# Hybrid decoder layer on one core: the first 512 streamed columns of w_in as four row pieces of full width, multiplied as each block of tokens arrives

## Chip, cores and metric

The kernel runs on one core of a Trainium2 chip. The metric is the device time of one execution in microseconds (us); lower is better. A core has a TensorE (PE), a VectorE (DVE), a ScalarE (ACT), a GpSimd (POOL), and queues that start transfers, of which SyncE's (SP) carries the weights.

## The reference, cut to what matters

One decoder layer for 512 tokens of width 1024. The normalised tokens are multiplied with one wide matrix `w_in`; its column groups are the queries, the keys and values of three attention branches (compressed, selected, window), gates, and the inputs of an mLSTM. The compressed branch reads the keys and values of 31 overlapping blocks of 32 tokens, adds a position row, and sends them through two small matrices.

```python
h = rmsnorm(x, g_mix)                        # x * rsqrt(mean(x*x) + EPS) * g
z = h @ w_in                                 # split by IN_SIZES:
# q 512 | kc 128, vc 128 | ks 128, vs 128 | kw 128, vw 128 | gates 24 | mLSTM ...
def compress_blocks(tok_g, w1, w2, pe):
    idx = CMP_STRIDE * jnp.arange(n_cmp)[:, None] + jnp.arange(CMP_LEN)[None, :]
    blk = tok_g[:, :, idx] + pe
    flat = blk.reshape(b, g, n_cmp, CMP_LEN * d)
    return jax.nn.gelu(flat @ w1) @ w2
```

Behind them come attention, mLSTM, a mixture of 16 experts and per-layer embeddings. The change touches none of these; they take the time from about 70 us to the end.

## The kernel before, in words

**Tokens.** The 512 tokens are four blocks `b` of 128. Each block of x (`xs`) is loaded, its sum of squares formed by ScalarE (`square`), its scale by a chain of small VectorE operations (`rstd` for one block, `rstd_cols` for blocks 2 and 3 at once), and VectorE multiplies it by scale and g_mix (line 372). g_mix is one row (`grow`) that TensorE spreads over 128 partitions (`gmb`, line 320). `rows_t` then transposes the block by eight TensorE transposes into the PSUM tiles `tp` (line 376), and `parts` copies these into a high part `hTh` (ScalarE, line 383) and a rest `hTl` (VectorE, line 385).

**Weights.** `Stream` brings the pieces of `w_in` and of the compression weights (`w_ck`, `w_cv`) in a fixed order into four raw buffers (`rawWR`), and splits each into a high part `whWS` (ScalarE, lines 97 and 103) and a rest `wlWS` (VectorE, lines 100 and 106, or POOL, line 108) in one of four split buffers. A split buffer is free again when the last product with it is done. Each product of the reference is three TensorE products: hTh·wh, hTl·wh, hTh·wl.

**The steps and their order.** `ORDER` lists the pieces: `z2` (kc and vc, columns 512 to 767), `z3` (ks and vs, 768 to 1023), `z4` (kw, vw, gates; 288 columns, three pieces by rows), `z0`, `z1` (queries), and `c0`, `c1`, the first compression product for keys and for values, four pieces each. z2 and z3 are two pieces each: 512 rows by 256 columns. z2 is multiplied block by block while the blocks arrive (`tok_mm_late`, `z2_mm`); z3 follows for all four blocks at once. What is done with a finished step is in generators that are advanced between the pieces: `finish_c2` copies z2 (`zt`), turns it (rope), transposes it on TensorE (line 526), copies that to `TT` (lines 532, 534), adds the position rows (`tb`, line 580), and splits the result into `bhl` (lines 581, 582), which `c0` (line 589) reads. `z1_out` does it for the keys and values of z3 and z4 (`kz`, `v`, line 547; key transposes, line 557; `khh`, `kll`). `angles` makes the tables for rope (`trig`), for which ScalarE loads another function table and POOL negates a part; POOL then starts the transfer of `w2s`, which VectorE copies to `w2d` (line 569).

**PSUM.** The pool `PM` has three banks named `mm`, `PA` two each of `tp` and `S`, `PO` one `o`. z2 adds up in two `mm` banks, z3 in two `S` banks, z4 in two of each: it can start in a bank only when that bank's former content has been read.

`after(x)` and `issue_after(x)` only fix an order: what stands under them comes behind x in the program. Line numbers of the profile are those of the kernel it belongs to.

Of the kernel before, what the change touches and what calls it, by code (L numbers as in the profile page):

```python
# [19 lines left out]
P = 128  # L20
S = 512
# [111 lines left out]
def tile_hybrid(ctx, tc, x, p, positions, g_mix, w_in, b_if, w_ck1, w_ck2, pe_ck, w_cv1, w_cv2, pe_cv,  # L133
# [157 lines left out]
    def z1_acc(c):  # L291
        names = {2: ["mm"] * 2, 3: ["S"] * 2, 4: ["mm", "mm", "S", "S"], 0: ["mm"] * 2, 1: ["S"] * 2}[c]
        acc = [(PM if nm == "mm" else PA).tile([P, 512], F32, name=nm) for nm in names]
        if c == 4:
            return acc, [t[:, :288] for t in acc]
        return acc, [acc[b // 2][:, (b % 2) * 256:(b % 2) * 256 + 256] for b in range(NB)]

    acc2 = z1_acc(2)
    with tc.tile_pool(name="start", bufs=1) as sp:
# [54 lines left out]

        def z2_mm(b):
            for h in range(2):
                with tc.issue_after(tr_.ins) if h else nullcontext():
                    tok_mm(acc2[1], 4 * h, 4 * h + 4, *w2_[h], 256, 2, [b])
# [79 lines left out]
        tpc = PM.tile([P, 512], F32, name="mm")  # L438
        T.transpose(tpc[:, :92], rows, ident[:92, :92])
# [49 lines left out]
    def z1_mm(c, h, dst):  # L489
        with tc.issue_after(front_.ins) if (c, h) == (3, 0) else nullcontext():  # L490
            wh, wl = st.get(("z", c, h))
        if c == 4:
            tok_mm(dst, *K4[h], wh, wl, 288, 1)
        else:
            tok_mm(dst, 4 * h, 4 * h + 4, wh, wl, 256, 2)

    def z1_out(c, acc, j):
        for _ in range(1):
# [19 lines left out]
            elif c == 2:  # L518
                z = zp.tile([P, 2, 256], F32, name="zt")
                A.activation(z, acc[j].rearrange("p (b n) -> p b n", b=2), AF.Copy)  # L520
                rope(z[:, :, 0:128].rearrange("p b (h d) -> p b h d", h=2), j, 2, zp)
# [13 lines left out]
            else:  # L535
# [121 lines left out]
    def begin(g, wait):  # L657
        next(g)
        later.append([wait, g, wait])

    for o in ORDER:
        c = int(o[1])
        if o[0] == "z":
            h = done_z.get(c, 0)
            done_z[c] = h + 1
            if h == 0:
                accs[c] = z1_acc(c) if c != 2 else acc2
            if c != 2:
                z1_mm(c, h, accs[c][1])
                advance(5)  # L670
            if h == (2 if c == 4 else 1):
                if c == 2:
                    begin(finish_c2(), WAIT[0])
                else:
                    for j in range(2):
                        begin(z1_out(c, accs[c][0], j), WAIT[1])
                if c == 4:
                    nsa_gates()
# [1015 lines left out]
```

## Time and profile before

| | us |
|---|---|
| median of 3 runs (lowest to highest) | 709.89 (709.51 to 711.25) |
| the profiled execution | 711.02 |
| its span in the profile | 709.3 |
| PE busy in the span | 684.3 |
| DVE busy | 563.2 |
| ACT busy | 436.0 |
| POOL busy | 130.4 |

The span is that of the profiled execution; the difference between it and the 711.02 lies around the span. Busy times of several engines overlap. An engine's share is a mean over stages that have different limits: of the 709 us, the change concerns the first 70.

### The profile page before, as it was taken

How to read it: one execution, taken by the hardware profiler on the slowest of the kernel's cores; microseconds unless marked ns; L12 is line 12 of the kernel's file. 1: busy time of each engine (PE TensorE's matmuls, PEld its weight loads, DVE VectorE, ACT ScalarE, POOL GpSimd, SP SyncE). 2: the span in 40 equal slices, each digit the busy share in tenths (PEclk: the TensorE clock that was granted, in tenths of full speed). 3: DMA queues.
4: the chain of work that ended last, by engine and by line, in shares of the span. 5: the costliest groups of instructions: out<-in, count | busy, mean ns of one | idle time of the engine just before them, and what ended most of it. 6: DMA issues, size and time to landing. Idle time of an engine off the chain costs nothing.

```text
span 709.3 us, 11568 instructions
## 1 busy us (share of the span) xinstructions
PE 684.3 (96%) x3913; PEld 584.6 (82%) x3913; DVE 563.2 (79%) x1427; ACT 436.0 (61%) x848; POOL 130.4 (18%) x184
## 2 busy tenths in 40 slices
PE   7989989999999999999999999999999999999995
PEld 5989976889999998888888888876788888887784
DVE  5877989888777758888884673668999999986986
ACT  6447746576666666665553332326999999986642
POOL 5010023333334220000000001222222222110000
PEclk9999999999999999999999999999999999999998
DMA  8424551222121212332219438944999999607511
GB/s 267 124 73 140 167 140 32 85 65 61 31 60 30 61 31 64 87 79 71 83 38 354 146 119 266 375 154 157 388 394 362 355 329 365 245 31 269 191 63 60
DMA packets 83152, 113.72 MB, mean 160 GB/s; under 512 B 9553, under 2 KB 52129, under 8 KB 83090
## 3 DMA queue, kind: packets, MB, share of 16 engines
q1 hardware_dynamic: 73344, 97.14, 41.3%
q0 software_dynamic: 5648, 11.53, 4.5%
q10 hardware_dynamic: 4098, 4.30, 1.8%
q8 instruction: 31, 0.51, 0.3%
q14 instruction: 31, 0.25, 0.1%
HBM read 108.41 MB, written 12.58 MB: 171 GB/s over the span
## 4 chain that ended last, share of the span: by engine, by line
PE 79%; DVE 8%; DMA 6%; ACT 4%; issue 2%; POOL 1%; ACTq 0%; POOLq 0%; DVEq 0%
PE mm L945 12%; PE S L1476 11%; PE mm L271 10%; PE mm L1648 6%; PE mm L1501 6%; PE mm L1117 6%; PE mm L768 3%; PE mm L1281 3%; PE S L271 2%; PE tp L862 2%; DMA wr<-in_w_re 2%; PE S L841 2%; PE tp L1462 2%; DVE wlWS L106 1%; ACT whWS L103 1%
## 5 line engine op out<-in xcount | busy, mean ns | idle before, releaser
L106 DVE TENSOR_TENSOR wlWS<-rawWR,whWS 128x1024 fp32r<-128x1024 f32 (+2 forms) x78 | 89.5, 1153 | 28.6 <-ACT whWS L103 27.5
L103 ACT ACTIVATE whWS<-rawWR 128x1024 fp32r<-128x1024 f32 (+2 forms) x79 | 82.3, 1050 | 43.0 <-PE S L271 8.5
L106 DVE TENSOR_TENSOR wlWS<-rawWE,whWS 128x1024 fp32r<-128x1024 f32 x58 | 69.1, 1221 | 3.7 <-ACT whWS L103 2.4
L103 ACT ACTIVATE whWS<-rawWE 128x1024 fp32r<-128x1024 f32 x58 | 60.6, 1071 | 5.1 <-PE S L1476 4.5
L271 PE MATMUL mm<-whWS,hTl 128*128 128x256 f32 (+1 forms) x200 | 59.3, 296 | 1.4 <-DVE hTl L385 1.4
L271 PE MATMUL mm<-wlWS,hTh 128*128 128x256 f32 (+1 forms) x200 | 59.1, 296 | 0.0
L271 PE MATMUL mm<-whWS,hTh 128*128 128x256 f32 (+1 forms) x200 | 59.1, 296 | 0.0
L945 PE MATMUL mm<-hTh,whWS 128*128 128x512 f32 x128 | 50.3, 393 | 0.0
L945 PE MATMUL mm<-hTh,wlWS 128*128 128x512 f32 x128 | 50.0, 391 | 0.0
L945 PE MATMUL mm<-hTl,whWS 128*128 128x512 f32 x128 | 50.0, 391 | 0.0
L852 POOL TENSOR_SCALAR pr<-pr,sm 128x128 f32<-128x128 f32 (+3 forms) x64 | 35.2, 564 | 78.1 <-DVE sm L850 36.4
L1476 PE MATMUL S<-whWS,tgh 128*128 128x512 f32 x120 | 48.6, 405 | 0.0
L1476 PE MATMUL S<-wlWS,tgh 128*128 128x512 f32 x120 | 47.8, 398 | 0.1
L1476 PE MATMUL S<-whWS,tgl 128*128 128x512 f32 x120 | 47.3, 394 | 0.0
L846 ACT ACTIVATE pr<-pr,sm 128x128 f32<-128x128 f32 (+3 forms) x64 | 35.4, 555 | 16.9 <-DVE sm L844 16.8
L271 PEld LDWEIGHTS mm<-whWS,hTl 128*128 128x128 f32 x200 | 38.6, 193 | 1.7 <-DVE hTl L385 1.6
L271 PEld LDWEIGHTS mm<-wlWS,hTh 128*128 128x128 f32 x200 | 38.6, 193 | 0.0
L271 PEld LDWEIGHTS mm<-whWS,hTh 128*128 128x128 f32 x200 | 38.5, 193 | 0.1
L108 POOL TENSOR_TENSOR wlWS<-rawWR,whWS 128x384 fp32r<-128x384 f32 (+1 forms) x17 | 24.8, 1460 | 72.4 <-ACT whWS L103 67.5
L865 ACT ACTIVATE ph<-tp 128x512 fp32r<-128x512 f32 (+1 forms) x48 | 25.1, 523 | 20.4 <-PE tp L862 20.1
L842 DVE CUSTOM_DVE_ANT_0 pr<-S,strip 128x128 f32<-128x128 f32 (+3 forms) x64 | 29.3, 485 | 3.9 <-PE S L841 3.4
L1506 POOL DMA_INDIRECT y_dram<-ye,gidx x16 | 20.8, 1299 | 61.9 <-ACT aeh L1490 58.8
(490 smaller groups left out, 2076.6 us busy)
## 6 DMA issues: line engine op xcount, KB each, us to landing
rawWE<-in_w_e SPq DMA_DIRECT2D x59, 512.0 KB, 9.9
rawWR<-in_w_in SPq DMA_DIRECT2D x40, 512.0 KB, 3.9
mT<-in_w_e SPq DMA_DIRECT2D x22, 512.0 KB, 12.6
rawWR<-in_w_e SPq DMA_DIRECT2D x13, 512.0 KB, 10.4
rawWR<-in_w_out SPq DMA_DIRECT2D x8, 512.0 KB, 4.3
yy<-y_dram SPq DMA_DIRECT2D x8, 512.0 KB, 5.4
rawWR<-in_w_ck SPq DMA_DIRECT2D x4, 512.0 KB, 3.9
rawWR<-in_w_cv SPq DMA_DIRECT2D x4, 512.0 KB, 5.4
```

The lines of the kernel that those rows point to most:

```text
L103: self.last_hi = self.nc.scalar.activation(h[:, :n], flat, AF.Copy)
L106: self.last = self.nc.vector.tensor_tensor(l[:, :c], flat[:, :c], h[:, :c].bitcast(F32), OP.subtract)
L271: T.matmul(dst[b], a[:, kk, b * P:(b + 1) * P], w[:, kk - k0, :n], start=(kk == 0 and i == 0 and b % share == 0), stop=(kk == NK - 1 and i ...
L842: V.tensor_tensor_reduce(pr[:, hh, :n], s_[:, :n], strip[:, 512 - q0:640], 0.125, -3.0e38, OP.add, OP.max, sm[:, 0, hh:hh + 1])
L846: A.activation(pr[:, hh, :n], pr[:, hh, :n], AF.Exp, bias=sm[:, 1, hh:hh + 1], accum_out=sm[:, 2, hh:hh + 1])
L852: G.tensor_scalar(pr[:, hh, :n], pr[:, hh, :n], sm[:, 3, hh:hh + 1], 1.0, op0=OP.mult, op1=OP.mult)
L865: A.activation(ph[:, :nj], tp[:, :nj], AF.Copy)
L945: T.matmul(ps, w[:, k], a[:, k], start=(k == 0 and i == 0), stop=(k == NK - 1 and i == 2))
L1117: T.matmul(ps, w[:, k, f * P:(f + 1) * P], a[:, k], start=(k == 0 and i == 0), stop=(k == 3 and i == 2))
L1476: T.matmul(ps, a[:, 2 * m + k], w[:, k], start=(m == 0 and k == 0 and i == 0), stop=(m == 3 and k == 1 and i == 2))
L1501: T.matmul(acc[c], a[:, k], w[:, 0, c * 512:(c + 1) * 512], start=(k == 0 and i == 0), stop=(k == 1 and i == 2))
L1648: T.matmul(acc, a[:, k], w[:, 0, lo:hi], start=(k == 0 and i == 0), stop=(k == NK - 1 and i == 2))
```

## The change

The 512 columns of z2 and z3 are now four pieces `zz` 0 to 3 of 256 rows by 512 columns. `zz_mm` multiplies one of them with one block into the accumulator `accz[b]` (two `mm`, two `S`), 512 wide. All of it happens as the blocks arrive, so z2 and z3 no longer stand in `ORDER`, and their outputs (`finish_c2`, `z1_out(3)`) are begun ahead of z4. The low halves of zz0, zz1 and zz2 are POOL's, that of zz3 VectorE's; before, only that of z2's first piece was POOL's. The row of g_mix is now started second on SP's queue, before it was second on ScalarE's. Ten transposes on nothing (`keep_warm`, before 14) are made ahead of the g_mix products instead of behind them, and `gmb` lies in an `mm` and an `o` bank. The two small transposes for `trig` and `cols` go to `tp` banks. zt is copied in four pieces 256 wide, before two of 512.

```diff
-N_WARM = 14
+N_WARM = 10
...
-ORDER = "z2 z2 z3 z3 z4 z4 c0 z4 c0 c0 z0 c0 z0 c1 z1 c1 z1 c1 c1".split()
+ORDER = "z4 z4 c0 z4 c0 c0 z0 c0 z0 c1 z1 c1 z1 c1 c1".split()
...
+    for m in range(4):
+        st.add(("zz", m), [(0, 512, wall[:, 2 * m:2 * m + 2, 512:1024])], [P, 2, 512], *first)
...
+    def zz_mm(b, m, terms):
+
+        wh, wl = zw[m]
         for i in terms:
             a, w = ((hTh, wh), (hTl, wh), (hTh, wl))[i]
-            for kk in range(k0, k1):
-                m = T.matmul(dst[b], a[:, kk, b * P:(b + 1) * P], w[:, kk - k0, :n],
-                         start=(kk == 0 and i == 0 and b % share == 0),
-                         stop=(kk == NK - 1 and i == 2 and b % share == share - 1), skip_group_check=True)
-        return m
+            for kk in range(2):
+                last = T.matmul(accz[b], a[:, 2 * m + kk, b * P:(b + 1) * P], w[:, kk], start=(m == 0 and i == 0 and kk == 0),
+                                stop=(m == 3 and i == 2 and kk == 1), skip_group_check=True)
+        return last
...
-    acc2 = z1_acc(2)
+    accz, zw = z1_acc(4)[0], []
...
-                A.dma_start(grow, g_mix)
+                nc.sync.dma_start(grow, g_mix)
             if b < 2:
                 st._load()
-        keep_warm(N_WARM)
-
-        gmb = [PA.tile([P, 512], F32, name="S") for _ in range(2)]
+                st._load()
+        gm_ = keep_warm(N_WARM)
+
+        gmb = [PM.tile([P, 512], F32, name="mm"), PO.tile([P, 512], F32, name="o")]
         for c in range(2):
-            T.matmul(gmb[c], ones, grow[:, c * 512:(c + 1) * 512], start=True, stop=True)
+            with after(gm_):
+                gm_ = T.matmul(gmb[c], ones, grow[:, c * 512:(c + 1) * 512], start=True, stop=True)
...
-            w2_.append(st.get(("z", 2, 0)))
+            for m in range(2):
+                zw.append(st.get(("zz", m)))
+        ps0, xs_, tr_ = rows_t(0, None, gm_)
+        with after(st.last_hi):
+            hi_, lo_ = parts(0, ps0, None)
+        with after(hi_):
+            sq_ = square(1)
+        with after(lo_):
+            rstd(rst[:, 1:2], ss[:, 1:2], sp)
+        with after(sq_):
+            zw.append(st.get(("zz", 2)))
+        st.late_low = []
+        with after(st.last_hi):
+            zw.append(st.get(("zz", 3)))
+        (low_,), st.late_low = st.late_low, None
+        st.pool_from, st.split_ahead = D, 1
...
         with after(st.last_hi):
-            sq_ = square(1)
-        ps0, xs_, tr_ = rows_t(0, None)
-        with after(xs_):
-            made = rstd(rst[:, 1:2], ss[:, 1:2], sp)
-        with after(sq_):
-            hi_, lo_ = parts(0, ps0, made)
-        st.late_low = []
-        with after(hi_):
-            w2_.append(st.get(("z", 2, 1)))
-        (low_,), st.late_low = st.late_low, None
-        st.pool_from, st.split_ahead = D, 1
-        with after(st.last_hi):
-            for b in (2, 3):
-                sq_ = square(b)
-        tok_mm_late(acc2[1], 0, 4, *w2_[0], 256, 2, 0, (0, 1, 2))
-        m_ = tok_mm_late(acc2[1], 4, 8, *w2_[1], 256, 2, 0, (0, 1))
+            sq_ = square(2)
+        for i in range(3):
+            for m in range(2):
+                zz_mm(0, m, (i,))
+        for i in range(3):
+            m_ = zz_mm(0, 2, (i,))
         ps1, xs_, tr_ = rows_t(1, lo_, m_)
         with after(xs_):
-            xs_ = low_()
+            low_ = low_()
         with after(tr_):
-            tok_mm_late(acc2[1], 4, 8, *w2_[1], 256, 2, 0, (2,))
-        with after(xs_):
-            made = rstd_cols(rst[:, 2:4], ss[:, 2:4], sp, 2)
+            zz_mm(0, 3, (0, 1, 2))
         with after(sq_):
-            hi_, lo_ = parts(1, ps1, made)
+            hi_, lo_ = parts(1, ps1, low_)
+        with after(hi_):
+            square(3)
+        with after(lo_):
+            rstd_cols(rst[:, 2:4], ss[:, 2:4], sp, 2)
         for b in (2, 3):
-            psb, xs_, tr_ = rows_t(b, lo_ if b == 2 else xs_)
-            z2_mm(b - 1)
-            hi_, lo_ = parts(b, psb, None)
+            psb, xs_, tr_ = rows_t(b, lo_)
+            for m in range(4):
+                with after(tr_ if m > 1 else None):
+                    zz_mm(b - 1, m, (0, 1, 2))
+            hi_, lo_ = parts(b, psb, xs_)
         with after(lo_):
             trig = angles()
-        z2_mm(NB - 1)
+        for m in range(4):
+            zz_mm(NB - 1, m, (0, 1, 2))
         front_ = lo_
...
-                A.activation(z, acc[j].rearrange("p (b n) -> p b n", b=2), AF.Copy)
+                for b in range(2):
+                    A.activation(z[:, b], acc[2 * j + b][:, 0:256], AF.Copy)
...
-        gens = [z1_out(2, accs[2][0], j) for j in range(2)]
+        gens = [z1_out(2, accz, j) for j in range(2)]
...
+    begin(finish_c2(), WAIT[0])
+    for j in range(2):
+        begin(z1_out(3, accz, j), WAIT[1])
```

TensorE, around the transposes of block 1 (tile `tp` from `xs`). Before, with block 0: `mm` is z2's accumulator, `wh`/`wl` numbers 154/155 are z2's first piece, 196/197 its second.

```order
L282 MATMUL mm_92<-whWS_196,hTh_76 128x256 [waits Activation_49]
...
L282 MATMUL mm_92<-whWS_196,hTl_77 128x256 [waits DVE_49]
...
L376 MATMUL tp_227<-ident_78,xs_109 128x128 [waits DMAHW5_49,DVE_49,PE_49]
...
L282 MATMUL mm_92<-wlWS_197,hTh_76 128x256 [waits DVE_49]
...
L271 MATMUL mm_92<-whWS_154,hTh_76 128x256 [waits Activation_49]
```

The same place after the change; the numbers of `wh`/`wl` are 152/153 for zz0, 159/160 for zz1, 193/194 for zz2, 199/200 for zz3.

```order
L286 MATMUL mm_92<-wlWS_153,hTh_76 128x512 [waits Pool_49]
L286 MATMUL mm_92<-wlWS_153,hTh_76 128x512
L286 MATMUL mm_92<-wlWS_160,hTh_76 128x512 [waits Pool_49]
L286 MATMUL mm_92<-wlWS_160,hTh_76 128x512
L286 MATMUL mm_92<-whWS_193,hTh_76 128x512 [waits Activation_49]
L286 MATMUL mm_92<-whWS_193,hTh_76 128x512
L286 MATMUL mm_92<-whWS_193,hTl_77 128x512 [waits DVE_49]
L286 MATMUL mm_92<-whWS_193,hTl_77 128x512
L286 MATMUL mm_92<-wlWS_194,hTh_76 128x512 [waits Pool_49]
L286 MATMUL mm_92<-wlWS_194,hTh_76 128x512
L375 MATMUL tp_234<-ident_78,xs_113 128x128 [waits DMAHW6_49,DVE_49,PE_49]
```

The transposes of block 1 stood ahead of the last low half's products; now they stand behind the products with POOL's third low half.

TensorE, from z4 to c0, after the change: `mm_510`, `mm_511`, `S_512`, `S_513` are z4's accumulators for blocks 0 to 3, `tp_604` the c2 transposes, `tp_672` the key transposes, `mm_758` z0's accumulator, `o_627` c0's.

```order
L274 MATMUL mm_510<-whWS_514,hTh_76 128x288 [waits Activation_49]
...
L274 MATMUL mm_511<-whWS_514,hTh_76 128x288 [waits DVE_49]
...
L274 MATMUL S_512<-whWS_514,hTh_76 128x288 [waits DVE_49,PE_49]
...
L536 MATMUL tp_604<-ident_78,zt_456 128x128 [waits DMAHW0_49,DMASW0_49,PE_49]
...
L567 MATMUL tp_672<-ident_78,qs_490 128x128 [waits DVE_49,PE_49]
...
L274 MATMUL mm_758<-whWS_744,hTh_76 128x256 [waits Activation_49]
...
L599 MATMUL o_627<-whWS_562,bhl_454 128x256 [waits DVE_49]
...
L599 MATMUL o_627<-whWS_760,bhl_454 128x256 [waits Activation_49]
L274 MATMUL mm_758<-wlWS_745,hTh_76 128x256 [waits DVE_49]
```

Before, the c2 transposes stood behind z3 and ahead of all of z4; now 72 of z4's 96 products come first, and c0's first product follows 24 products of z4, the key transposes and four products of z0 later.

VectorE, after the change, where z4's banks come free: `mm_92`, `mm_93`, `S_94`, `S_95` are `accz` 0 to 3, `v1` the values of z3, `wlWS_629` the low half of z4's third piece.

```order
L106 TENSOR_TENSOR wlWS_629<-rawWR_202,whWS_628 128x576 [waits DMAHW1_49,DMAHW0_49,PE_49]
...
L557 TENSOR_TENSOR v1_436<-mm_92,v1_436 128x2x64 [waits Activation_49]
L491 TENSOR_TENSOR zt_466<-rope_a_469,rope_b_470 128x2x2x16 [waits DVE_49]
L557 TENSOR_TENSOR v1_436<-mm_93,v1_436 128x2x64 [waits Activation_49]
L579 COPY w2d_452<-w2s_449 128x256 [waits DMASW0_49]
L487 TENSOR_TENSOR rope_a_483<-kz_476,trig_379 128x2x2x8
...
L557 TENSOR_TENSOR v1_436<-S_94,v1_436 128x2x64 [waits Activation_49]
```

Before, the same reads of z3's banks (line 547) stood there too, but z4 could begin in `mm` banks that z2 had left long before; now the copy of `w2d` stands ahead of the read of `S_94`.

## Rows read from the trace of the kernel before

**Rows 1.** The page, its first line.
```profile
span 709.3 us, 11568 instructions
```
**Rows 2.** Windows of 100 us: length, busy time and count by engine, TensorE's granted clock, DMA.
```profile
200.00:300.00 100.00, 100.00 (x694) 92.40 (x694) 75.17 (x221) 62.85 (x145) 22.31 (x40) 1.00 0.21 54
```
**Rows 3.** TensorE's waits, 0 to 62 us: total, times, longest.
```profile
PE S L271 <- DVE v L547: 2.0, 1, 2.0
PE mm L271 <- DVE hTl L385: 1.4, 1, 1.4
```
**Rows 4.** Windows of 2 us, columns as in rows 2 (PE, PEld, DVE, ACT, POOL).
```profile
16.00:18.00 2.00, 1.11 (x8) 0.68 (x6) 1.76 (x12) 2.00 (x4) 0.00 (x0) 1.00 0.44 76
...
46.00:48.00 2.00, 0.10 (x1) 0.13 (x2) 1.97 (x7) 0.48 (x1) 0.00 (x0) 1.00 0.41 143
48.00:50.00 2.00, 2.00 (x12) 2.00 (x13) 1.79 (x5) 1.46 (x3) 0.00 (x0) 0.70 0.00 0
50.00:52.00 2.00, 2.00 (x10) 2.00 (x10) 2.00 (x3) 0.52 (x1) 0.00 (x0) 0.50 0.00 0
52.00:54.00 2.00, 2.00 (x16) 2.00 (x15) 1.33 (x3) 0.00 (x0) 0.54 (x2) 0.95 0.26 30
```
**Rows 5.** Timeline, 6 to 18 us: start, busy, engine, line, output and input.
```profile
6.86 2.35 POOL L108 TENSOR_TENSOR wlWS<-rawWR,whWS 128x1024 fp32r<-128x1024 f32 x1 [4.17 <-ACT whWS L103]
...
8.59 1.06 ACT L364 ACTIVATE junk<-xs 128x1024 f32<-128x1024 f32 x1 [1.81 <-DMA xs<-in_x]
...
12.75 0.66 POOL L461 MEMSET strip<- 128x640 f32 x1
...
14.23 0.32 POOL L462 TENSOR_SCALAR_AFFINE_SELECT strip<-strip 128x128 f32<-128x128 f32 x1
...
15.23 1.03 PE L376 MATMUL tp<-ident,xs 128*128 128x128 f32 x8
...
16.12 0.16 DVE L231 TENSOR_SCALAR rs_n<-ss 128x2 f32<-128x2 f32 x1
...
17.69 0.16 DVE L241 SCALAR_TENSOR_TENSOR rst<-rs_n 128x2 f32<-128x2 f32 x1
```
**Rows 6.** The chain that ended last, in order of time: start, length, what.
```profile
52.98 2.38 PE S L271 x18
...
62.29 5.76 PE mm L271 x48
...
270.21 2.74 PE mm L945 x12
```
**Rows 7.** Timeline, TensorE at 41 us.
```profile
41.01 1.03 PE L526 MATMUL tp<-ident,zt 128*128 128x128 f32 x8
```
**Rows 8.** Timeline, 30 to 39 us, ScalarE, POOL and VectorE.
```profile
30.54 1.28 ACT L350 ACT_TABLE_LOAD   x1
...
34.23 0.80 POOL L566 DMA_DIRECT2D w2s<-in_w_ck  x1 [0.74 <-DMA rawWR<-in_w_ck]
...
38.67 0.29 DVE L569 COPY w2d<-w2s 128x256 f32<-128x256 f32 x1 [3.47 <-DMA w2s<-in_w_ck]
```
**Rows 9.** Timeline, 43 to 68 us, VectorE and ScalarE.
```profile
43.51 0.75 DVE L534 COPY TT<-tp 64x256 f32<-64x256 f32 x2
...
48.59 1.19 DVE L582 TENSOR_TENSOR bhl<-tb,bhl 128x992 fp32r<-128x992 f32 x1 [0.17 <-ACT bhl L581]
...
62.15 1.28 ACT L634 ACT_TABLE_LOAD   x1
...
67.02 1.22 DVE L106 TENSOR_TENSOR wlWS<-rawWR,whWS 128x1024 fp32r<-128x1024 f32 x1
```
**Rows 10.** The source line 108, all of the run, and the timeline near 90 us.
```profile
L108 POOL TENSOR_TENSOR wlWS<-rawWR,whWS x17: 997/1642/2352, 6.9 to 228.3; 128x384 fp32r<-128x384 f32 x16, 128x1024 fp32r<-128x1024 f32 x1
...
88.28 0.22 DVE L478 TENSOR_TENSOR rope_a<-zt,trig 128x64 f32<-128x64 f32 x1
...
91.28 1.05 DVE L478 TENSOR_TENSOR rope_a<-zt,trig 128x64 f32<-128x64 f32 x1
```

More of the change, by code (lines that the diff above doesn't have):

```diff
@@ L157, in tile_hybrid @@
     win = w_in[0].rearrange("(h k p) n -> h p k n", h=2, p=P)
-    ZC = {2: 512, 3: 768, 4: 1024, 0: 0, 1: 256}
+    ZC = {0: 0, 1: 256}
     wall = w_in[0].rearrange("(k p) n -> p k n", p=P)
     wck = [w[0].rearrange("(m p) n -> p m n", p=P) for w in (w_ck1, w_cv1)]
+    for m in range(4):
+        st.add(("zz", m), [(0, 512, wall[:, 2 * m:2 * m + 2, 512:1024])], [P, 2, 512], *first)
     seen = {}
@@ L263, in keep_warm @@
         for _ in range(n):
-            T.transpose(warm[:, 0:P], ident, ident)
+            last = T.transpose(warm[:, 0:P], ident, ident)
+        return last
     def tok_mm_steps(dst, k0, k1, wh, wl, n, share, blocks=range(NB)):
@@ L275, in tok_mm_steps @@
                         yield
-    def tok_mm_late(dst, k0, k1, wh, wl, n, share, b, terms):
+    def zz_mm(b, m, terms):
+        wh, wl = zw[m]
         for i in terms:
             a, w = ((hTh, wh), (hTl, wh), (hTh, wl))[i]
-            for kk in range(k0, k1):
-                m = T.matmul(dst[b], a[:, kk, b * P:(b + 1) * P], w[:, kk - k0, :n],
-                         start=(kk == 0 and i == 0 and b % share == 0),
-                         stop=(kk == NK - 1 and i == 2 and b % share == share - 1), skip_group_check=True)
-        return m
+            for kk in range(2):
+                last = T.matmul(accz[b], a[:, 2 * m + kk, b * P:(b + 1) * P], w[:, kk], start=(m == 0 and i == 0 and kk == 0),
+                                stop=(m == 3 and i == 2 and kk == 1), skip_group_check=True)
+        return last
     def tok_mm(*args):
@@ L291, in z1_acc @@
     def z1_acc(c):
-        names = {2: ["mm"] * 2, 3: ["S"] * 2, 4: ["mm", "mm", "S", "S"], 0: ["mm"] * 2, 1: ["S"] * 2}[c]
+        names = {4: ["mm", "mm", "S", "S"], 0: ["mm"] * 2, 1: ["S"] * 2}[c]
         acc = [(PM if nm == "mm" else PA).tile([P, 512], F32, name=nm) for nm in names]
@@ L323, in angles @@
             V.tensor_copy(posf, posr)
-            tpp = PM.tile([P, 512], F32, name="mm")
+            tpp = PA.tile([P, 512], F32, name="tp")
             T.transpose(tpp[:, :NB], posf, ident[:NB, :NB])
@@ L352, in angles @@
             return trig
[L355 to L358, printed above, removed]
         rst = const.tile([P, NB], F32, name="rst")
-        prev, w2_ = None, []
         def square(b):
@@ L402, in tile_hybrid @@
         with after(st.last_hi):
-            sq_ = square(1)
-        ps0, xs_, tr_ = rows_t(0, None)
-        with after(xs_):
-            made = rstd(rst[:, 1:2], ss[:, 1:2], sp)
-        with after(sq_):
-            hi_, lo_ = parts(0, ps0, made)
-        st.late_low = []
-        with after(hi_):
-            w2_.append(st.get(("z", 2, 1)))
-        (low_,), st.late_low = st.late_low, None
-        st.pool_from, st.split_ahead = D, 1
-        with after(st.last_hi):
-            for b in (2, 3):
-                sq_ = square(b)
-        tok_mm_late(acc2[1], 0, 4, *w2_[0], 256, 2, 0, (0, 1, 2))
-        m_ = tok_mm_late(acc2[1], 4, 8, *w2_[1], 256, 2, 0, (0, 1))
+            sq_ = square(2)
[4 more added lines that the diff above has]
+            m_ = zz_mm(0, 2, (i,))
         ps1, xs_, tr_ = rows_t(1, lo_, m_)
         with after(xs_):
-            xs_ = low_()
+            low_ = low_()
         with after(tr_):
-            tok_mm_late(acc2[1], 4, 8, *w2_[1], 256, 2, 0, (2,))
-        with after(xs_):
-            made = rstd_cols(rst[:, 2:4], ss[:, 2:4], sp, 2)
+            zz_mm(0, 3, (0, 1, 2))
         with after(sq_):
-            hi_, lo_ = parts(1, ps1, made)
-        for b in (2, 3):
-            psb, xs_, tr_ = rows_t(b, lo_ if b == 2 else xs_)
-            z2_mm(b - 1)
-            hi_, lo_ = parts(b, psb, None)
+            hi_, lo_ = parts(1, ps1, low_)
[3 more added lines that the diff above has]
+            rstd_cols(rst[:, 2:4], ss[:, 2:4], sp, 2)
+        for b in (2, 3):
+            psb, xs_, tr_ = rows_t(b, lo_)
[3 more added lines that the diff above has]
+            hi_, lo_ = parts(b, psb, xs_)
         with after(lo_):
             trig = angles()
-        z2_mm(NB - 1)
+        for m in range(4):
+            zz_mm(NB - 1, m, (0, 1, 2))
         front_ = lo_
         cols = const.tile([P, 92], F32, name="cols")
-        tpc = PM.tile([P, 512], F32, name="mm")
+        tpc = PA.tile([P, 512], F32, name="tp")
         T.transpose(tpc[:, :92], rows, ident[:92, :92])
@@ L489, in z1_mm @@
     def z1_mm(c, h, dst):
-        with tc.issue_after(front_.ins) if (c, h) == (3, 0) else nullcontext():
+        with after(front_ if (c, h) == (4, 0) else None):
             wh, wl = st.get(("z", c, h))
@@ L540, in z1_out @@
                 kz = zp.tile([P, 2, P], F32, name="kz")
-                src = [acc[2 * j + b][:, :256] if c == 4 else acc[j][:, b * 256:(b + 1) * 256] for b in range(2)]
+                src = [acc[2 * j + b][:, :256] if c == 4 else acc[2 * j + b][:, 256:] for b in range(2)]
                 for b in range(2):
@@ L666, in tile_hybrid @@
             if h == 0:
[L667 to L670, printed above, removed]
+                accs[c] = z1_acc(c)
+            z1_mm(c, h, accs[c][1])
+            advance(5)
             if h == (2 if c == 4 else 1):
[L672 to L676, printed above, removed]
+                for j in range(2):
+                    begin(z1_out(c, accs[c][0], j), WAIT[1])
                 if c == 4:
```

## The prediction, made before the result was known

> **What bounds the kernel now.** I read the page first. The span is 709.3 us [rows 1] and the profiled execution as a whole took 711.02, 1.1 above the median of 709.89; TensorE is the bound nearly everywhere, and from 200 to 300 us it is busy all the time [rows 2]. So a microsecond that TensorE wins or loses in the first 70 us comes out at the end one for one, unless a later wait swallows it. The first 100 us are where the change works, so next I read TensorE's waits up to 62 us: 2.0 us of z4 for a VectorE operation of the z3 output, and 1.4 us for hTl of block 1 [rows 3]. The windows show the price behind the 2.0: TensorE stands from 46 to 48, and then the granted clock is 0.70, 0.50 and 0.95 in the next three windows [rows 4], that is 2 x (0.30 + 0.50 + 0.05) = 1.7 us of lost work at the lower level (1.2 instead of 2.4 GHz).
>
> **The front, up to the start of z4.** The work itself: before, z2 and z3 are 192 products 256 wide at 0.120 each (48 in 5.76 [rows 6]) = 23.0 us; after, 96 products 512 wide at 0.228 (12 in 2.74 [rows 6]) = 21.9 us. That is 1.1 us won. The rest hangs on where the transposes of block 1 can start. Before, they start at 15.23 [rows 5], ahead of the late low half of z2's second piece. After, they stand behind the low products of zz2 in TensorE's order, and that low half is POOL's third. POOL: the low half of zz0 ends at 6.86 + 2.35 = 9.2 [rows 5]. zz1 is now the third transfer of the queue; the third one before, block 1 of x, was there at 8.6 [rows 5], so its high half is done at about 9.6 and its low half at 12.0. The strip and vcm operations follow, 1.8 us (12.75 to 14.55 [rows 5]), and zz2's low half runs from about 13.9 to 16.3 (zz2's high half is ready at about 12.9, after square(1)). The transposes of block 1 then start at about 16.7, 1.5 later than before. From there: transposes of three blocks (1.03 for one [rows 5]), some 3.0; 78 products x 0.228 = 17.8; the two small transposes 0.3; and a wait of 0.5 before block 2, whose scale comes after hTh of block 1, a square (1.06) and the chain of rstd_cols (16.12 to 17.85, 1.7) [rows 5]. z4 starts at 16.7 + 21.6 = 38.3. Before, z3's products ended at 41.0, where the eight c2 transposes begin [rows 7], and z4 followed 0.8 later. So the front wins 41.0 - 38.3 = **2.7 us**. Bounds: 3.3 if POOL runs with no gap (block 1 at 16.1), and below nothing if POOL's low halves go slower. The row set beside them is 997 to 2352 ns for 17 of them, 16 of these only 384 wide [rows 10]; at the median, 1.64 us for 384, the 1024 wide ones would take 4.4 each and block 1 would start at 20.5, a loss of 1.1 instead of the gain. I take 2.35, since it is the row of the same size in the same stretch.
>
> The Trainium skill (GPSIMD Engine Reference, 1. Specifications) says that POOL shares its SBUF interfaces with VectorE and that they contend where a VectorE instruction has two SBUF inputs. By that rule the L100 for zz3, beside zz2's low half, goes slower or holds POOL, and it speaks against three low halves on POOL. The trace agrees as to VectorE: a rope operation with two SBUF inputs took 1.05 us beside POOL's L108, against 0.22 without it [rows 10]. By rule alone the front would give some of its 2.7 us back.
>
> **z4.** Its work is the same. Before it waited once, 2.0 us, and lost 1.7 at the low clock. After, z3 is no cover any more between the outputs of the first accumulators and z4, which needs their banks. Block 1 of z4 waits for v from accz[0] (L557), block 2 for v from accz[2]; in VectorE's order both stand behind the low half of z4's third piece and the rope of c2, the second also behind the copy of w2d, which waits for the transfer w2s. What ScalarE does ahead: the high halves of z4's first pieces and c0's first each wait for the last product of block 3 with zz0, zz1, zz2 (four split buffers), so the third ends at about 37.9; table load 1.28 [rows 8], sine, z4's third high half: 40.2. VectorE: low half until 41.3, nine rope operations, v at 42.5. TensorE has run out at 38.3 + 18 x 0.132 (18 in 2.38 [rows 6]) = 40.7: **1.9 us** of wait. w2s is issued by POOL behind the sine, at about 39.9 to 40.6 (before it stood idle 0.74 there [rows 8]), and takes 4.4 (34.23 to 38.67 [rows 8]): 44.3 to 45.0, then w2d, four rope operations, v: 45.2 to 46.0, I take 45.6. TensorE stands from 43.8: **1.8 us**. Together 3.7, as much as the 2.0 + 1.7 of before: 0.0, as long as the clock stays up. It is unlikely to stay: 3.7 us of idle in 5 us is more than the 2.0 that made it fall [rows 4]. So **+1.7** for a second fall of the same size; lower bound 0.
>
> **From c2 to c0.** Before, c2's transposes began at 41.01 [rows 7], and bhl was complete at 48.59 + 1.19 = 49.78 [rows 9]: 8.8 us, all of it under z4's products and waits, so c0 never waited. After, they come behind 72 products of z4, with only 24 products of z4, the key transposes and four of z0 to cover: 3.2 + 1.0 + 0.95 + 0.5 = 5.6 us. With the same 8.8 c0 waits **3.2 us**. Bounds: with every operation tight, transposes 1.0 and then 43.51 to 49.78 [rows 9] = 6.3, it is 7.3 and the wait 1.7; upper, with c0's third low half in front, 4.0. Behind that, VectorE's order has z0's first low half behind bhl, two casts, ropes and the gate's operation, which waits for ScalarE's table load (1.28 [rows 9]); with its own 1.22 [rows 9] it is ready 3.8 us after bhl, while c0's 24 products (2.9) are over: **+0.9**. The wait of 3.2 lets the clock fall again, as after 2.0; of the 1.7 that this costs some two thirds lie under the 0.9 just counted: **+0.5** (0.2 to 1.2). From 69 us on the order is that of before.
>
> Warm transposes (10 for 14), their place ahead of the gmb products, and grow on the other queue: block 0's transposes can start earlier, but its products then wait for POOL's low halves, so all of it is inside the 16.7; nothing by itself (without that cover up to 2 us, which would be won, not lost). The copies of zt in four of 256 instead of two of 512 lie beside z4's first 18 products.
>
> Sum: -2.7 + 0.0 + 1.7 + 3.2 + 0.9 + 0.5 = **+3.6 us**, 711.02 + 3.6 for the profiled execution, and 709.89 + 3.6 = 713.5 on the median.
>
> **Rivals.** (1) The waits come, but the clock does not fall after z4's two waits, which are split by 1.2 us of work: +1.9, 711.8; with no fall at all +1.4, 711.3. For it: the 1.4 us wait at 17 us [rows 3] brought no fall: the window that holds it has a clock of 1.00 [rows 4]. (2) On the other side: z4's waits do not come, since v of accz is read before TensorE gets there. The place is ScalarE's row ahead of the sine; it decides if v from accz[0] is out by 40.7 and w2s has landed by 42.5, some 2 us ahead of my chain. Then 3.7 and 1.7 drop out: 3.6 - 5.4 = -1.8, 708.1; with a tight bhl chain (wait 1.7 instead of 3.2, no fall) -3.8, 706.1. Against it: the buffers of z4's pieces are freed only by block 3. (3) POOL's low halves go slower beside VectorE, so that block 1 starts 1 to 3.8 us later: 714.5 to 717.3. For it the spread in [rows 10]; against it the 2.35 of the one that is 1024 wide. (4) The front's gain meets the first bhl wait so exactly that nothing changes: part of (1).
>
> **How the numbers follow.** About 0.3% (2.1 us, 707.8 to 712.0) is what a measurement of this kernel can tell from no change. Forecast 0.38 (its own range 712.3 to 714.5); (1) 0.24, within 0.3%; (2) 0.30, of it 0.20 faster and 0.10 within; (3) 0.08. So faster 0.20, same 0.34, slower 0.46. The range goes from 707.0, inside (2), to 715.0, inside (3), and leaves out some 0.15.
>
> **What would show it.** Right: block 1's transposes at 16 to 17.5; z4's start near 38.3; two waits of z4 for L557, together 3 to 4.5 us, with a clock of 0.5 in a window behind them; c0's first product waiting 2.5 to 4 us for bhl's low half; c0's last eight products near 71.7 (before at 62.29 + 5.76 = 68.05 [rows 6]). Wrong: no wait at L599 for bhl, no second low-clock stretch, or POOL's 1024 wide low halves at 3 us and more.

## The result, and the profile after

The changed kernel takes 719.2 us (718.22 to 719.52, 4 runs), the kernel before 709.79 (709.51 to 711.25, 4 runs): the ratio is 1.0126, with a 95% interval of 1.0109 to 1.0144. It is slower, as forecast, but by 9.4 us and not by 3.6, and outside the range of 707.0 to 715.0. The profiled execution took 719.0, its span is 717.2, 7.9 more than [rows 1].

TensorE's waits up to 72 us, after the change (total, times, longest), in place of [rows 3]:

```profile
PE o L599 <- DVE bhl L592: 3.0, 1, 3.0
PE S L274 <- DVE kz L491: 2.4, 1, 2.4
PE mm L286 <- POOL wlWS L108: 2.3, 1, 2.3
...
PE mm L274 <- DVE v L557: 1.2, 1, 1.2
PE mm L286 <- ACT hTh L382: 0.9, 1, 0.9
PE mm L274 <- ACT whWS L103: 0.5, 1, 0.5
```

Three of them are the waits that were forecast: c0 for bhl (3.0), z4 for its banks (1.2 and 2.4; the second names the operation that ended last before it, `kz`, which stands on VectorE behind the copy of w2d). The wait for POOL is the one in the front. The windows of 2 us, columns as in [rows 4], show the granted clock behind the second and the third:

```profile
48.00:50.00 2.00, 0.91 (x4) 0.94 (x5) 1.92 (x13) 0.42 (x1) 0.00 (x0) 0.80 0.06 20
50.00:52.00 2.00, 2.00 (x10) 2.00 (x9) 0.83 (x5) 0.42 (x1) 0.00 (x0) 0.50 0.01 4
52.00:54.00 2.00, 2.00 (x14) 2.00 (x14) 0.00 (x0) 0.85 (x1) 0.00 (x0) 0.85 0.00 0
...
64.00:66.00 2.00, 0.00 (x0) 0.00 (x0) 1.97 (x4) 1.73 (x6) 0.00 (x0) 1.00 0.00 0
66.00:68.00 2.00, 1.81 (x8) 1.82 (x9) 1.91 (x6) 1.82 (x4) 0.00 (x0) 0.57 0.00 0
68.00:70.00 2.00, 2.00 (x13) 2.00 (x12) 1.97 (x9) 1.94 (x4) 0.00 (x0) 0.58 0.00 0
```

Each stretch costs 1.7 us (2 x (0.20 + 0.50 + 0.15) and 2 x (0.43 + 0.42), the length of a window times what is missing to a clock of 1.00). The front, in the timeline, answers to [rows 5]:

```profile
1.26 0.32 SPq L316 DMA_DIRECT2D grow<-in_g_mix  x1
...
1.63 0.90 SPq L77 DMA_DIRECT2D rawWR<-in_w_in  x2
...
8.22 1.06 ACT L103 ACTIVATE whWS<-rawWR 128x1024 fp32r<-128x1024 f32 x1 [2.72 <-DMA rawWR<-in_w_in]
...
9.36 4.71 POOL L108 TENSOR_TENSOR wlWS<-rawWR,whWS 128x1024 fp32r<-128x1024 f32 x2 [6.66 <-ACT whWS L103]
...
15.73 1.22 DVE L100 TENSOR_TENSOR wlWS<-rawWR,whWS 128x1024 fp32r<-128x1024 f32 x1
15.74 3.41 POOL L108 TENSOR_TENSOR wlWS<-rawWR,whWS 128x1024 fp32r<-128x1024 f32 x1
...
19.20 0.73 PE L286 MATMUL mm<-wlWS,hTh 128*128 128x512 f32 x2 [2.30 <-POOL wlWS L108]
...
19.78 1.04 PE L375 MATMUL tp<-ident,xs 128*128 128x128 f32 x8
```

ScalarE waits until 8.22 for the transfer of zz0; before, POOL's first low half could start at 6.86 [rows 5], now at 9.36. The first two take 2.35 each, the third 3.41, beside VectorE's L100. The transposes of block 1 start at 19.78, before at 15.23. Further on, the timeline from 41 us, in place of [rows 7 to 9]:

```profile
41.31 0.24 PE L448 MATMUL tp<-ident,rows 92*128 92x92 f32 x1
...
43.52 0.80 POOL L576 DMA_DIRECT2D w2s<-in_w_ck  x1 [0.73 <-DVE gph L451]
...
48.04 0.29 DVE L579 COPY w2d<-w2s 128x256 f32<-128x256 f32 x1 [2.57 <-DMA w2s<-in_w_ck]
...
49.09 0.47 PE L274 MATMUL S<-whWS,hTh 128*128 128x288 f32 x1 [2.44 <-DVE kz L491]
...
56.67 1.03 PE L536 MATMUL tp<-ident,zt 128*128 128x128 f32 x8
...
66.19 0.54 PE L599 MATMUL o<-whWS,bhl 128*128 128x256 f32 x1 [3.01 <-DVE bhl L592]
...
76.78 0.28 PE L599 MATMUL o<-wlWS,bhl 128*128 128x256 f32 x1
```

c0's last product starts at 76.78. Before, it started at 68.72:

```profile
68.72 0.28 PE L589 MATMUL o<-wlWS,bhl 128*128 128x256 f32 x1
```

So 8.1 us are lost by then, all of the 7.9; from that product to the end of the span there are 640.4 us now and 640.6 before.

### The profile page after: what moved, and what is told of

It is laid out like the page before. It is cut to its first block, busy times and chain, and to the rows that moved or that the text cites. A ratio compares the mean times of both kernels' runs of the same rounds, so it can differ in the third digit from the quotient of the medians.

```text
span 717.2 us, 11371 instructions
## 1 busy us (share of the span) xinstructions
PE 687.7 (96%) x3813; PEld 581.7 (81%) x3813; DVE 562.1 (78%) x1425; ACT 436.1 (61%) x850; POOL 135.7 (19%) x186
## 5 line engine op out<-in xcount | busy, mean ns | idle before, releaser
L106 DVE TENSOR_TENSOR wlWS<-rawWR,whWS 128x1024 fp32r<-128x1024 f32 (+2 forms) x76 | 87.0, 1153 | 30.4 <-ACT whWS L103 29.4
L274 PE MATMUL mm<-whWS,hTh 128*128 128x256 f32 (+1 forms) x176 | 51.7, 294 | 1.7 <-DVE v L557 1.2
L274 PE MATMUL mm<-whWS,hTl 128*128 128x256 f32 (+1 forms) x176 | 51.8, 294 | 0.0
L274 PE MATMUL mm<-wlWS,hTh 128*128 128x256 f32 (+1 forms) x176 | 51.6, 294 | 0.0
L108 POOL TENSOR_TENSOR wlWS<-rawWR,whWS 128x384 fp32r<-128x384 f32 (+1 forms) x19 | 30.6, 1613 | 59.6 <-ACT whWS L103 54.8
L874 ACT ACTIVATE ph<-tp 128x512 fp32r<-128x512 f32 (+1 forms) x48 | 25.1, 522 | 20.3 <-PE tp L871 19.8
L274 PEld LDWEIGHTS mm<-whWS,hTh 128*128 128x128 f32 x176 | 33.4, 190 | 2.3 <-DVE v L557 1.5
L274 PEld LDWEIGHTS mm<-whWS,hTl 128*128 128x128 f32 x176 | 33.4, 190 | 0.1
L274 PEld LDWEIGHTS mm<-wlWS,hTh 128*128 128x128 f32 x176 | 33.4, 190 | 0.0
```

The costliest lines, as they stand in the source:

```text
L106: self.last = self.nc.vector.tensor_tensor(l[:, :c], flat[:, :c], h[:, :c].bitcast(F32), OP.subtract)
L108: self.nc.gpsimd.tensor_tensor(l[:, c:n], flat[:, c:], h[:, c:n].bitcast(F32), OP.subtract)
L874: A.activation(ph[:, :nj], tp[:, :nj], AF.Copy)
```

## The experiments

All are edits of the changed kernel, but one. The kernel before, measured again beside them, had medians of 710.2 to 711.1 us; the changed kernel was not measured again, so differences from its 719.2 are good to about 1 us. The theory after the first look: four losses in three places. The front loses to the transfer of zz0 (A) and to POOL's third low half (C); z4 to the copy of w2d (D); c0 to the late transposes of c2 (E). Rivals are named with each.

**The row of g_mix back on ScalarE's queue.**

```diff
-                nc.sync.dma_start(grow, g_mix)
+                A.dma_start(grow, g_mix)
```

> The changed kernel with the row of g_mix back on ScalarE's queue; nothing else differs. Theory A (the row, second on SyncE's queue, holds back the weight transfers behind it): zz0 arrives near 5.7 us instead of 8.2, POOL's first low half starts near 6.9 instead of 9.4, the transposes of block 1 start 2 to 2.5 us earlier than 19.8, and the time falls by 2 to 2.5 us from 719.2. Theory B (two wide pieces ahead of block 1 share the bandwidth, whatever the row does): zz0 stays near 8 us and the time stays within 1 us.

717.1 us (714.89 to 719.71, 6 runs), ratio to before 1.0093 (1.0066 to 1.0120). In its timeline zz0 no longer makes ScalarE wait, and the third low half is POOL's alone at first:

```profile
5.76 1.06 ACT L103 ACTIVATE whWS<-rawWR 128x1024 fp32r<-128x1024 f32 x1
...
6.90 2.35 POOL L108 TENSOR_TENSOR wlWS<-rawWR,whWS 128x1024 fp32r<-128x1024 f32 x1 [4.21 <-ACT whWS L103]
...
13.97 2.40 POOL L108 TENSOR_TENSOR wlWS<-rawWR,whWS 128x1024 fp32r<-128x1024 f32 x1
...
15.44 2.02 DVE L100 TENSOR_TENSOR wlWS<-rawWR,whWS 128x1024 fp32r<-128x1024 f32 x1
...
16.99 1.03 PE L375 MATMUL tp<-ident,xs 128*128 128x128 f32 x8
```

Theory A holds, B falls: one row of 4 KB ahead of the weights makes zz0 2.5 us late. Block 1 starts 2.8 us earlier, at 17.0, and z4 at 38.6 instead of 41.3. In this profile z4's second wait is 1.4 instead of 2.4, with no fall of the clock behind it, and the stretch at 0.50 behind c0's wait is longer (59 to 66 us). Whether the clock falls varies from run to run here: the mean granted clock is 0.992 in the fastest run and 0.986 in the slowest, and the time scatters by 4.8 us. The median is 2.1 below the changed kernel, as expected, and still above the forecast range.

**The same row in the kernel before.** The reverse edit, there alone (line 313 of the kernel before).

> The kernel before with one part of the change alone: the row of g_mix second on SyncE's queue. If the row holds back the weights behind it, z2's first piece is there near 8 us instead of 5.7, its POOL low half ends near 11.7, and as block 0's first products wait for it (13.8 before) there is room: time within 1 us of 709.8. If the two wide pieces were what delayed zz0, z2's first piece is there at 5.7 as before.

712.97 us (710.54 to 714.98, 5 runs), ratio 1.0036 (1.0011 to 1.0061). z2's first piece is late in this kernel too; its high half, first without the edit, then with it:

```profile
5.72 1.06 ACT L103 ACTIVATE whWS<-rawWR 128x1024 fp32r<-128x1024 f32 x1
```

```profile
8.02 1.06 ACT L103 ACTIVATE whWS<-rawWR 128x1024 fp32r<-128x1024 f32 x1 [2.47 <-DMA rawWR<-in_w_in]
...
9.16 2.37 POOL L108 TENSOR_TENSOR wlWS<-rawWR,whWS 128x1024 fp32r<-128x1024 f32 x1 [6.47 <-ACT whWS L103]
...
15.66 1.03 PE L376 MATMUL tp<-ident,xs 128*128 128x128 f32 x8
```

So it is the row and not the wide pieces. With a single low half on POOL most of it is covered: block 1 starts 0.4 later, not 2.8. The median rose by 2.8 over that of the kernel before beside it, not by the 1 us at most that was expected. The three slower executions have a mean granted clock of 0.991 to 0.993, the two at 710.6 one of 0.994 and 0.996; why it fell in three of five was not traced. The profiled execution has a span of 708.8, below that of before, with the same wait in z4 (1.9) and no fall of the clock.

**zz2's low half on VectorE.**

```diff
+        st.pool_from = D
         with after(sq_):
             zw.append(st.get(("zz", 2)))
```

> The changed kernel with the low half of zz2 on VectorE instead of POOL. Theory C (POOL's third low half, behind two others and the strip operations and slowed to 3.4 us, is what block 1 waits for): TensorE's wait of 2.3 us for POOL goes, block 1's transposes start near 17 us, and the time falls by 2 to 3 us. Rival: VectorE's row is then as late (scale and product of block 1 behind the low half), transposes at 19 us or later, time within 1 us of 719.2.

715.6 us (714.42 to 716.44, 6 runs), ratio 1.0064 (1.0040 to 1.0088), 3.6 below the changed kernel. The wait for POOL is gone and block 1 starts at 17.16, though zz0 is as late as ever (8.33). Theory C holds; the rival falls. The front explains 2.6 of the 3.6; the rest was not traced. What now sets the start of block 1 is TensorE: it is busy from block 0's first product at 11.27 on, and the first eight products take some 0.45 us each, where later ones of the same size take 0.23. The granted clock reads 1.00 in these windows, so the rows do not say why. In the changed kernel the first eight are as slow, but the wait for POOL lies behind them.

**All low halves on POOL.** `late_low` and the call of `low_` are left out, so zz3's low half follows zz2's on POOL.

> The changed kernel with all four low halves on POOL, so that no low half of VectorE (two SBUF inputs) runs beside that of zz2. If POOL's 3.4 us for zz2's low half come from the L100 beside it, it takes 2.35 to 2.45 here and block 1's transposes start near 18.8 instead of 19.8; if they come from something else (the transfers of that stretch), it stays at 3.3 or more. zz3's low half is then ready near 20.6, so TensorE waits once more, up to 1 us; time 718 to 720.

One execution, 715.86 us. POOL's row and block 1:

```profile
15.84 4.70 POOL L108 TENSOR_TENSOR wlWS<-rawWR,whWS 128x1024 fp32r<-128x1024 f32 x2
...
18.82 1.04 PE L375 MATMUL tp<-ident,xs 128*128 128x128 f32 x8
```

Two low halves in 4.70, 2.35 each, without L100 beside them: the 3.41 came from VectorE. The transfers of that stretch, the other candidate, were no fewer (a DMA share of 0.98 from 16 to 18 us, 0.80 in the changed kernel). TensorE waits 1.5 us for zz2's low half instead of 2.3, and not at all for zz3's, where up to 1 was expected. The time is below the 718 to 720 expected, though z4 starts only 0.9 earlier: z4's second wait is 1.4 instead of 2.4, and the clock stays at 1.00 behind it.

**The copy of w2d behind bhl.** It is made in `cmp_in(0)`, after bhl.

```diff
-    V.tensor_copy(w2d, w2s[:, 0, :, None, :].to_broadcast([P, 2, 2, 64]))
...
+        if kv == 0:
+            V.tensor_copy(w2d, w2s[:, 0, :, None, :].to_broadcast([P, 2, 2, 64]))
         blks[kv] = PO.tile([P, 512], F32, name="o")[:, :256]
```

> The changed kernel with the copy of w2d moved behind bhl in VectorE's order, so that nothing in front of z4's banks waits for the transfer w2s. Theory D (that transfer makes z4's second wait and with it the fall of the clock): the wait of 2.4 us falls under 0.5, the granted clock stays at 1.0 from 48 to 54, and the time falls by 3 to 4 us. Rival (the wait only moves): c0 waits for bhl by as much more, 5 us instead of 3, and the time stays within 1 us.

714.89 us (714.14 to 715.4, 7 runs), ratio 1.0055 (1.0034 to 1.0076): 4.3 below the changed kernel. The windows in which the clock had fallen:

```profile
48.00:50.00 2.00, 2.00 (x17) 2.00 (x17) 0.64 (x2) 1.34 (x2) 0.00 (x0) 1.00 0.02 7
50.00:52.00 2.00, 2.00 (x17) 2.00 (x17) 1.01 (x1) 0.00 (x0) 0.00 (x0) 1.00 0.04 8
```

Theory D holds: the second wait is gone, and with it the low clock, 2.4 + 1.7 = 4.1. The wait for bhl stays at 3.0.

**c2's transposes earlier.** The second stage of finish_c2 comes after one piece of z4 instead of two.

```diff
-WAIT = 9, 13, 11.5
+WAIT = 4, 13, 11.5
```

> The changed kernel with the second stage of finish_c2 one piece of z4 earlier (its waiting time in the order 4 instead of 9): c2's transposes come behind 9 to 45 products of z4 instead of 72. Theory E (c0's wait of 3.0 us and the fall of the clock behind it come from c2 being transposed too late): the wait for bhl falls under 0.5, the clock stays at 1.0 from 62 to 72, and the time falls by 4 to 5 us from 719.2. Rival (VectorE's chain from TT to bhl ends no earlier, since the low halves of c0 stand in it): the wait stays above 2 us and the time within 1 us.

716.71 us (715.7 to 716.98, 4 runs), ratio 1.0094 (1.0075 to 1.0113): 2.5 less than the changed kernel, where theory E expected 4 to 5. Neither theory is met. The wait for bhl goes from 3.0 to 1.2, but others take its place; its waits:

```profile
PE tp L536 <- ACT v L556: 1.4, 1, 1.4
PE o L599 <- DVE bhl L592: 1.2, 1, 1.2
PE o L599 <- ACT whWS L103: 1.0, 1, 1.0
PE tp L567 <- DVE kll L573: 1.0, 1, 1.0
```

The transposes of c2, now early, wait for ScalarE; behind c0's first piece the key transposes wait for the casts to kll and c0's last piece for its high half, both of which stand behind one another on ScalarE and VectorE. The clock falls at 66 us, behind these, for 1.7 us as before. So c0 loses as much as in the changed kernel: 1.2 + 1.0 + 1.0 against 3.0 + 0.5, and the same 1.7. What was won lies in z4, where the waits are 1.4 (that of the c2 transposes) and 1.4 instead of 1.2 and 2.4, and the clock stays up; these 0.9 and the 1.7 are about the 2.5:

```profile
48.00:50.00 2.00, 2.00 (x15) 2.00 (x16) 1.85 (x11) 0.84 (x3) 0.00 (x0) 1.00 0.01 4
50.00:52.00 2.00, 2.00 (x18) 2.00 (x17) 1.25 (x3) 1.74 (x3) 0.00 (x0) 1.00 0.04 8
```

**Two edits: the row and the copy of w2d.**

> The changed kernel with two edits: the row of g_mix back on ScalarE's queue and the copy of w2d behind bhl; c2's second stage as in the changed kernel. The two losses are in different places, so they add: front 2.8 us less, z4's second wait and its fall of the clock 4 less, c0's wait of 3.0 and its fall remain. Expected 712 to 713 us against 719.2, about 2 above the kernel before. If the run with three edits (712.5) gained from the third at all, this one is 1 us or more slower than it.

713.48 us (712.18 to 714.04, 10 runs), ratio 1.0041 (1.0026 to 1.0057). The two gains nearly add: 5.7 of 9.4 us are won back, against 2.1 + 4.3 for each alone; the time is 0.5 above the range expected. What is left is c0's wait, 3.0, and the clock at 0.50 to 0.53 from 58 to 64 us and 0.76 in the window behind.

**Three edits: also the earlier c2.**

> The changed kernel with three edits together: row of g_mix back on ScalarE's queue, copy of w2d behind bhl, c2's second stage earlier. If the three losses are separate, they add: 2.8 us of the front, some 4 of z4, 4 to 5 of c0, so about 11 less than 719.2, 707 to 709, up to 1% faster than the kernel before. If they hide one another (one wait takes the place of the next), the sum stays under 8 and the time above 711.

712.47 us (711.56 to 713.78, 8 runs), ratio 1.0032 (1.0013 to 1.0051). It won 1.0 more, not 4 to 5 (the two intervals overlap): the same waits as in the run with the earlier c2 alone (1.4, 1.2, 1.0, 1.0). The second expectation is the one that came.

**Four edits: also zz2's low half on VectorE.**

> As the run with three edits, and zz2's low half on VectorE. With the row back, POOL's third low half ends near 16.4 and block 1's transposes start at 17.0; if VectorE is free for it at 13.3, they start up to 1 us earlier and the time falls by up to 1 us against the run with three edits; if VectorE's scale and product of block 1 then come late, no change or up to 1 us slower.

712.22 us (710.36 to 714.62, 12 runs), ratio 1.0024 (1.0013 to 1.0035): the same time as with three. Block 1 starts at 18.16, later than with three edits (17.09), but not for VectorE, whose product of block 1 is done at 17.1. zz1 came later in this execution. First the rows with three edits, then with four:

```profile
8.87 1.06 ACT L103 ACTIVATE whWS<-rawWR 128x1024 fp32r<-128x1024 f32 x1 [2.26 <-DMA rawWR<-in_w_in]
...
17.09 1.03 PE L375 MATMUL tp<-ident,xs 128*128 128x128 f32 x8
```

```profile
9.85 1.06 ACT L103 ACTIVATE whWS<-rawWR 128x1024 fp32r<-128x1024 f32 x1 [3.05 <-DMA rawWR<-in_w_in]
...
18.16 1.04 PE L375 MATMUL tp<-ident,xs 128*128 128x128 f32 x8
```

In all six profiles with the row back, zz2's low half on POOL or on VectorE, block 1 starts 8.2 to 8.3 us behind the start of zz1's high half, which varies from 8.77 to 9.92. So neither half of the expectation is shown. In this profile, the slowest of the twelve executions, the clock is 1.00 up to 120 us and falls at 122 and 654 us, where no edit reaches.

**z0's first piece ahead of c0.** With the two edits; `ORDER` begins z4 z4 z4 z0 c0 c0 c0 z0 c0.

> The two edits of the run before, and z0's first piece (48 products, 5.8 us) ahead of c0's first in the order, instead of an earlier c2. If c0's wait of 3.0 us and the fall of the clock behind it are only for want of cover, both go (wait under 0.5, clock 1.0 from 58 to 70) and the time falls by 4 to 5 us against the run with two edits: 707 to 709, faster than the kernel before by up to 0.5%. If z0's first piece is not split in time, TensorE waits for its low half instead and the time stays above 711.

712.11 us (710.51 to 714.71, 12 runs), ratio 1.0028 (1.0012 to 1.0045). The wait for bhl is gone and the clock is 1.00 from 52 us on, and still the time fell by 1.4 only. It is 712.11, above the 711 of the second half of the expectation, but not for z0's low half. With this order c2's transposes came behind 18 products of z4, and TensorE stood there:

```profile
42.00:44.00 2.00, 0.00 (x0) 0.00 (x0) 1.95 (x9) 0.77 (x5) 1.73 (x1) 0.84 1.03 325
44.00:46.00 2.00, 1.74 (x8) 1.77 (x9) 2.00 (x16) 0.46 (x2) 0.00 (x0) 0.50 0.68 204
46.00:48.00 2.00, 2.00 (x10) 2.00 (x9) 1.56 (x7) 0.96 (x3) 0.00 (x0) 0.50 0.02 5
48.00:50.00 2.00, 2.00 (x10) 2.00 (x10) 0.69 (x2) 0.12 (x1) 0.00 (x0) 0.50 0.00 0
50.00:52.00 2.00, 2.00 (x16) 2.00 (x16) 0.00 (x0) 0.94 (x1) 0.00 (x0) 0.95 0.03 8
```

A wait of 2.8 us and, in the time that TensorE was busy, a low clock of 0.50 x (1.74 + 2.00 + 2.00) + 2 x 0.05 = 3.0 took the place of the 3.0 and its clock. The transposes wait for `zt`, and VectorE is late with it:

```profile
41.37 2.39 DVE L451 TENSOR_SCALAR gph<-cols 128x8 f32<-128x8 f32 x1
...
41.89 1.84 POOL L581 MEMSET bhl<- 128x2048 f32 x1
...
44.26 1.08 PE L536 MATMUL tp<-ident,zt 128*128 128x128 f32 x4 [2.79 <-issue]
```

`gph` takes 0.17 in the changed kernel, where it comes ahead of POOL's issue of w2s. Here it comes behind, and it and the six rope operations that follow it end only at 43.76, just after POOL's memset (43.73). The run below shows the same (2.39, from 42.48; memset to 44.84). That POOL holds VectorE there is read from these rows; no run moved the memset.

**The same with z0's second piece behind c0's first.**

> As the run with z0's first piece ahead of c0, and z0's second piece behind c0's first. Same wait at bhl; the later pieces of c0 have 5.8 us more cover for their low halves. Within 1 us of that run if nothing waits there; up to 1 us faster if c0's second piece waited for its low half.

714.37 us (713.51 to 715.19, 6 runs), ratio 1.0058 (1.0036 to 1.0081). Slower than the run before it by 2.3, against both expectations; the transposes of c2 wait 2.8 here too, and block 1 started at 18.1 instead of 17.0. The latter is not the edit's doing: the front is the same, but zz1's high half began at 9.92 in this profile and at 8.82 in that of the run before. This profile also has a fall of the clock at 96 us. No version was faster than the kernel before, so none beats both.

## Why the prediction was right and wrong, point by point

**The front: the step that failed.** Forecast were 2.7 us won, measured are 0.3 lost (z4 starts at 41.3; z3's products ended at 41.0 before). From block 1's transposes to z4 the sum came out: 21.6 forecast, 41.34 - 19.78 = 21.6 measured. The start was wrong, 19.8 and not 16.7. The step that put "grow on the other queue" at "nothing by itself" failed: the sum counts zz1 as the third transfer of the queue, where the row makes it the fourth, and took the arrival of the first piece from the kernel before; with the row ahead of it on the queue it came 2.5 us later, at 8.2 (shown by the row alone, put back and put into the kernel before). That made POOL's chain start at 9.36 instead of 6.86. The third low half then began at 15.74 instead of 13.9, at the same time as VectorE's L100, and took 3.41 beside it, not 2.35; the time without L100 is 2.35 (run with all on POOL). These 1.8 and 1.1 are 2.9 of the 3.1 by which block 1 was late. With the row alone put back, the forecast chain comes out: third low half from 13.97 to 16.37 (forecast 13.9 to 16.3), block 1 at 16.99 (16.7), z4 at 38.6 (38.3). The prediction named the slower low half as a bound and a rival, but did not use it.

The Trainium skill (GPSIMD Engine Reference, 1. Specifications) says that POOL shares its SBUF interfaces with VectorE and that they contend where a VectorE instruction has two SBUF inputs. The trace agrees, on POOL's side too: 1.06 us more for the low half beside L100.

The bound of 20.5 for block 1 is itself too low: with low halves of 4.4 the 1.8 of strip operations still lie between the second and the third, which gives 22.3 and a loss of 2.9, not 1.1.

**z4: right in kind and in sum.** Forecast were waits of 1.9 and 1.8, together 3.7; measured are 1.2 and 2.4, together 3.7. That the two misses of 0.6 to 0.7 cancel is luck. Forecast for the fall of the clock 1.7, measured 1.7. The copy of w2d as the cause of the second is shown by its move.

**c0: right in place and size.** Forecast 3.2 for bhl, measured 3.0. From c2's transposes to bhl it took 9.5 instead of 8.8, with 6.5 to cover it instead of 5.6, of it the 0.5 of the wait named below. The wait for z0's low half (0.9) did not come, since c0 at the low clock took longer than that; the clock cost 1.7 in place of 0.9 + 0.5. A wait of 0.5 for z0's high half was not forecast.

**The sum.** Of the terms of the forecast 3.6, the front is 3.0 off, the two of c0 0.3, the wait of 0.5 is new, and bhl is 0.2 less: 7.2 of the 7.9 between the two profiled executions are so accounted for; 0.7 was not traced. The other 1.5 up to 9.4 lie for the most part in the kernel before, whose profiled execution was 1.2 above its median: it had the fall of the clock, which by their mean clock more than half of its later executions did not have (12 of 21, below). So the forecast's "as much as the 2.0 + 1.7 of before" probably credits more than the median holds. The front is thus about half of the 5.8 us between forecast and measurement; with the row alone put back the time is still 717.1.

**The rivals.** The one with POOL slower beside VectorE (block 1 later by 1 to 3.8 us, 714.5 to 717.3) had the right place and half of the cause; the late transfer was in none. The first, without a fall of the clock, and the second, without z4's waits, did not come.

## What to carry to other kernels

A small transfer put ahead of large ones on a queue is not free: look at what the first consumer behind it then waits for, and take no arrival time over from a kernel in which the queue's order was another. z3's products had covered the steps from z2's result to c0. Without them TensorE waited 1.2, 2.4 and 3.0 us and lost 3.4 more at the low clock, against 2.0 and 1.7 before. When such cover is gone, moving a late step helps less than it promises: the earlier c2 and the earlier z0 each took one wait away, and others of about its size came in its place. So the whole row of each engine up to the next joint has to be followed. And one profile is one execution: a late transfer or a fall of the clock in a place that no edit touches can be as large as the gain that is looked for.

## What the runs showed of the hardware

**The fall of the clock is not the same in all executions of one kernel.** A z4 wait of some 2.0 us was followed by a clock of 0.50 in the profile of before [rows 4] and by none in the kernel before with the row moved (1.9, clock 1.00). The profiles without a fall in TensorE's busy time have a mean clock of 0.996, those with one that costs 1.7 us 0.993 to 0.994, those with more or longer ones 0.991 to 0.993. The 21 executions of the kernel before that ran beside the experiments with two edits and with z0's pieces moved differ in the same way: with a mean clock of 0.996 or more they took 708.25 to 711.96 us (12, ten of them up to 710.01), with 0.994 or less 710.31 to 713.72 (9). Falls of 1.7 us each also came at 122 us (three and four edits), 654 us (four edits) and 96 us (the last run).

**A row of 4 KB on one partition** delayed the 512 KB behind it on its queue: their first reader started at 8.22 instead of 5.76 us and, in the kernel before, at 8.02 instead of 5.72.

**POOL and VectorE.** In the three runs in which the two 1024 wide low halves began within 0.02 us of one another (the changed kernel, the late copy of w2d, the earlier c2), VectorE's took 1.22 and POOL's 3.40 to 3.42 instead of 2.35. In the five in which POOL's began 1.0 to 1.5 us ahead, POOL's took 2.38 to 2.40 and VectorE's 2.02 to 2.51. The delayed one takes about its own time and what is left of the other's: with the row back 16.37 - 15.44 = 0.93 and 1.22 make 2.15, and 2.02 were measured.
